# Strassen's weight sums by accumulating DMA in a transformer block's MLP on one Trainium2 core

## The chip, the cores and the metric

The kernel runs on one core of one Trainium2 chip. Its time is the device time of that core in microseconds; the number for a kernel is the median of several runs. Engines are named as in the profile: PE multiplies matrices, DVE and POOL do elementwise work, ACT does copies and functions, SP issues transfers. Each has its own queue of instructions, which it works off in order; they wait for one another by semaphores.

## The reference

One layer of a flow-matching backbone on 640 tokens (128 of a prompt, 512 of an image) of width 1024: a mixer (neighbourhood attention and a gated DeltaNet), then an MLP. Only the MLP matters here; its hidden width is 4096.

```python
def _ffn_sub(x, shift, scale, gate, w_pre, w_post, w1, w2):
    h = _rms(x, w_pre) * (1 + scale) + shift
    f = jnp.square(jax.nn.relu(h @ w1)) @ w2
    return x + gate * _rms(f, w_post)
```

## The kernel before

Everything is in fp32, and every product is made of three: each operand is split into a rounded part (hi, a cast on ACT) and a rest (lo, a subtraction on DVE), and hi·hi, hi·lo and lo·hi are added up in a PSUM bank. `split` (lines 165 to 172) does it for a weight tile of 128 x 1024, line 170 the cast and line 171 the subtraction, into one of four pairs of buffers (`whi`, `wlo`).

The MLP begins at line 1113. The 4096 hidden features go in eight groups of 512. For each group, `ff1` makes the hidden features from all tokens and `ff2` multiplies them by their rows of the second matrix and adds the result to sums `R` in SBUF. Both use Winograd's form of Strassen's scheme: the weights of a group are four quadrants, 512 KB each, and seven products of sums of quadrants take the place of eight plain ones. The plain way is used for the first product of group 0 (`ff1_first`), the second product of group 7 (in the code at the end, under the pool `fin`), and the prompt's tokens (`prompt` in `ff2`).

The loop at line 1294 runs `ff1(g)`, then `ff2(g-1)`, then `fops` of group g's features, which makes the operands of the next `ff2`: four sums of feature quadrants on POOL (lines 1224 to 1230) and their splits. So one turn of the loop, called a group here, holds a whole `ff1` and a whole `ff2`: 168 matrix instructions of 128 x 320 and 108 of 128 x 512.

Per group four quadrants are loaded for each half (line 162, SP's queue) into a pool of five `raw` buffers. Sums of quadrants are made by `sm` on POOL (line 1125): S1, S2 and S3 in `ff1`, T1, T2 and T3 in `ff2`, and the fourth forms S4 and T4 in place of S2 and T2 (lines 1197 and 1268). They lie in two buffers named `sm` that rotate. `ff1_first` uses the same two buffers eight times for its relu (`rl`, lines 1145 to 1149). DVE adds each product to what it belongs to: line 1178 for `ff1`, line 1241 (`collect`, into `R`) for `ff2`; `done` (line 1174) squares the relu.

The order on each engine is set by a scheduler that simulates the program when it is built; the code's order is its starting point. The program up to the MLP is the same in both kernels.

Of the kernel before, what the change touches and what calls it, by code (L numbers as in the profile page):

```python
# [18 lines left out]
P = 128  # L19
# [11 lines left out]
# packed constants: name -> (pack, offset, width); pack 1 is used at the start only  # L31
# [65 lines left out]
def body(ctx: ExitStack, tc: tile.TileContext, I, O, dbg=None):  # L97
# [41 lines left out]
    def newton_rsqrt(pool, x, n, tag, post=1.0):  # L139
        """1/sqrt(x) for x [P, n] > 0, times post."""  # L140
# [14 lines left out]
    behind = []  # loads wait for this one's issue  # L155
    rawp = [None, 0]  # the stage's pool for raw weights, and its buffers
# [8 lines left out]
    def split(raw, kt, n, pool=None, eng=V):  # L165
        """[P, kt, n] as the sum of two float32r parts"""
        pool = pool or wpool
        hi = pool.tile([P, 1024], F32R, tag="whi", name="whi")
        lo = pool.tile([P, 1024], F32R, tag="wlo", name="wlo")
        S.copy(hi, raw)  # L170
        eng.tensor_tensor(lo, raw, hi.bitcast(F32), op=ALU.subtract)  # L171
        return [x.rearrange("p (k n) -> p k n", k=kt) for x in (hi, lo)]
# [4 lines left out]
    def load_tok(src, n, pool=None):  # L177
        """a weight block whose columns stream: by input tile (hi, lo)"""
# [7 lines left out]
    def mm3(out, pairs):  # L186
        """out = sum of a^T b over (a_hi, a_lo, b_hi, b_lo)."""
# [24 lines left out]
    def ada_rows(c, pool):  # L212
        """256 columns of the modulation as rows: partial sums at partitions 32g + r."""
# [11 lines left out]
    def ada_cols(c, kk, dst, bcol, nsel, pool):  # L225
        """shift and (1 + scale) * norm_pre of features kk*128..+128 as columns"""
# [9 lines left out]
    def ada_gate(which, j, pool):  # L236
        """gate rows times the weight of the norm to DRAM"""
# [10 lines left out]
    def gate_bcast(which, pool):  # L248
        """(g + b) * norm_post over the partitions: [P, group, 1024]"""
# [38 lines left out]
    ab = cv.tile([P, 64], F32, tag="ab", name="ab")  # a_log, dt_bias, exp(a_log)  # L288
    cw = cv.tile([P, 60], F32, tag="cw", name="cw")

    with tc.tile_pool(name="xp", bufs=1, side="right") as xp:
        # x for now where the queries and keys will be, by halves of the features; scaled and
        # transposed to where the values will be and to a tile of the stage
# [4 lines left out]
        with tc.manual_schedule(engines={mybir.EngineType.SP}):  # L298
# [22 lines left out]
            # features as the modulation comes in; each one's products with w_z go out at once  # L321
# [42 lines left out]
    rawp[:] = [cv, 4]  # L364
    behind.append(lastd[0])
    # z: token-major, times dn_norm and its silu (twice)
# [8 lines left out]
    # b, a: features on 32 partitions, four partial sums side by side; then token-major  # L375
# [20 lines left out]
    # beta and g  # L396
# [8 lines left out]
    # softplus(x) = max(x, 0) + 2 atanh(u / (2 + u)), u = exp(-|x|)  # L405
# [25 lines left out]
    # cumulative decays  # L431
# [26 lines left out]
    # q, k, v: feature-major projection, convolution, silu, token-major  # L458
# [6 lines left out]
    for x in range(3):  # L465
# [32 lines left out]
        if x < 2:  # L498
            # values carry a factor 2 from the silu
# [45 lines left out]
    def transpose4(src, out, ps=None):  # L545
        """[tok, (a, d)] to [d, a, tok]"""
# [5 lines left out]
    def transpose8(src, tag):  # L552
        """[tok, (h, dir, d)] to [(dir, d), h, tok]"""
# [8 lines left out]
    def decay(m, d, mv, stat, lower):  # L562
        """exp of the sum of g over the open/closed run between p and f; exactly 0 outside the triangle"""
# [31 lines left out]
    def prep(mf, mb, buf):  # L595
        """everything of a pair of (tile, direction) units that doesn't need the state"""
# [3 lines left out]
        for d, m in ((0, mf), (1, mb)):  # L600
            known = m in seen  # the products of a tile serve both directions
# [5 lines left out]
            # upper: j on partitions, i >= j on columns  # L607
# [22 lines left out]
        # keys and queries times the decay from the chunk's start (and beta backward), both directions side by side  # L630
# [13 lines left out]
        Y = dp.tile([P, 16, 16], F32, tag="Yd", name="Yd")  # (column, unit)  # L644
# [8 lines left out]
        # packed: the diagonal 32 x 32 block of each row  # L653
# [7 lines left out]
        # 16 -> 32: Y12 = -Y11 U12 Y22 (the first 16 rows of U's block hold U12)  # L661
# [17 lines left out]
        # 32 -> 64  # L679
# [34 lines left out]
    def step(si, pr, St, first, last=False):  # L714
        """one chunk of both directions; St: [P (dir, dk), h, dv] or None for zero"""
# [3 lines left out]
        # right sides: v forward, beta v backward  # L719
# [37 lines left out]
        # output: q S and (q k^T) v_new  # L757
# [24 lines left out]
    def finish_o(ot, hv):  # L782
        """rms norm over each head, times dn_norm and the silu of z; feature-major to DRAM"""
# [60 lines left out]
    def fill():  # L844
        """dense work beside the DeltaNet"""
# [4 lines left out]
    def ahead(f, offset, *args):  # L850
        """f's instructions go before waiting ones of the filler"""
# [44 lines left out]
    with (  # L896
# [26 lines left out]
        for hp in range(HP):  # L923
# [3 lines left out]
            for mi in range(2):  # L927
# [5 lines left out]
                if mi == 0:  # L933
                    qb = at0.tile([P, T], F32, tag="qb", name="qb")  # context, then blocks of 16 columns
# [10 lines left out]
            # blocks of 16 columns of the grid, then the context  # L945
            for b in range(5):
                nk = 384 if b < 4 else 128
                po_ = None
                for hq in range(2):
# [7 lines left out]
                    if b < 4:  # L957
# [9 lines left out]
                        # negative scores and their minimum  # L967
# [28 lines left out]
    TG = [(0, 3), (3, 5)]  # token tiles side by side  # L996
# [7 lines left out]
    def load_wo(n, pool):  # L1004
        """the next n pieces of w_out: (hi, lo) by input tile, in fours"""
# [5 lines left out]
    if True:  # L1011
# [7 lines left out]
        for i in (1, 0):  # L1019
            if i == 0:  # L1020
# [4 lines left out]
                # m (and later h2 in its place): by token tile  # L1025
# [4 lines left out]
            for c in range(4):  # L1030
# [3 lines left out]
                for mi in range(2):  # L1034
# [3 lines left out]
                    for t0, t1 in TG:  # L1038
# [5 lines left out]
                        # twice the sigmoid times the branch  # L1044
# [8 lines left out]
    # output projection (of twice the merged branches), residual, second norm: by token tiles  # L1053
# [4 lines left out]
    with (  # L1058
# [6 lines left out]
        for t in range(5):  # L1065
# [28 lines left out]
            for kk in range(2):  # L1094
# [3 lines left out]
                # h2 takes the place of m  # L1098
# [347 lines left out]
```

## Time and profile before

| | us |
|---|---|
| median of 3 runs (1233.77 to 1238.07) | 1233.88 |
| span of the profiled execution | 1234.3 |
| DVE busy in it | 948.5 |
| POOL busy in it | 493.2 |
| ACT busy in it | 478.7 |

A row of the page's fifth part reads: line, engine, operation, output <- inputs, shape, count, then busy time, mean of one, and the idle time of the engine just before such instructions with what ended it. L171 stands for every weight split, whatever stage it belongs to; the tile on the right of the arrow (`raw`, `S`, `T`) tells whether a plain quadrant or a sum was split. The two costliest groups of the MLP on DVE and POOL:

```
L171 DVE TENSOR_TENSOR wlo<-T,whi 128x1024 fp32r<-128x1024 f32 x28 | 54.4, 1947 | 0.6 <-ACT whi L170 0.6
L1125 POOL TENSOR_TENSOR T<-raw 128x1024 f32<-128x1024 f32 x14 | 37.1, 2651 | 68.5 <-DVE wlo L171 37.8
```

### The profile page before, as it was taken

To read this page: it belongs to the slowest core of one execution; us is meant where nothing else is said; L and a number is where in the kernel's file an instruction comes from. 1 tells how busy PE (TensorE), PEld (TensorE's weight loads), DVE (VectorE), ACT (ScalarE), POOL (GpSimd) and SP (SyncE) were. 2 spreads that over 40 slices of the span, in tenths; PEclk is the share of its full clock that TensorE was granted. 3 is DMA by queue.
4 is the path that set the end of the run, shared out by engine and by line. 5 is a ranking of instruction groups with operands and counts; after the bars stand their busy time and mean duration, and the time that the engine had idled before them with its cause. 6 is when DMAs were issued, how large, how long until landed. Compare 5 with 4: busy or idle time off the path is not lost. (4 is left out here: it accounts for less than half of the span.)

```text
span 1234.3 us, 24857 instructions
## 1 busy us (share of the span) xinstructions
PE 1132.2 (92%) x10111; PEld 993.8 (81%) x10111; DVE 948.5 (77%) x1689; ACT 478.7 (39%) x910; POOL 493.2 (40%) x322
## 2 busy tenths in 40 slices
PE   5999799899989899898999899989989989898896
PEld 3789799778777788887877899988878879796875
DVE  6568996575677675735655667899999999999996
ACT  5434344342423233224435253545443434344322
POOL 1442425150542110402310415756564656556555
PEclk9999999898989899999999999989999999999999
DMA  9721033434425433645332562022213123221405
GB/s 337 266 93 50 1 102 133 149 129 137 144 77 176 141 109 111 215 132 194 98 104 105 178 246 102 18 71 67 85 52 103 57 81 103 69 86 52 155 33 136
DMA packets 61313, 144.87 MB, mean 117 GB/s; under 512 B 12384, under 2 KB 26000, under 8 KB 61200
## 3 DMA queue, kind: packets, MB, share of 16 engines
q1 hardware_dynamic: 38528, 108.66, 26.0%
q10 hardware_dynamic: 22672, 34.64, 9.0%
q8 instruction: 79, 1.29, 0.4%
q14 instruction: 34, 0.28, 0.1%
HBM read 122.02 MB, written 21.25 MB: 116 GB/s over the span
## 5 line engine op out<-in xcount | busy, mean ns | idle before, releaser
L190 PE MATMUL ps_mm<-hhi,whi 128*128 128x320 f32 x576 | 186.8, 324 | 2.5 <-DVE gbn L244 2.0
L192 PE MATMUL ps_mm<-hhi,wlo 128*128 128x320 f32 x576 | 183.5, 319 | 0.3 <-issue 0.3
L191 PE MATMUL ps_mm<-hlo,whi 128*128 128x320 f32 x576 | 183.5, 319 | 0.0
L171 DVE TENSOR_TENSOR wlo<-raw,whi 128x1024 fp32r<-128x1024 f32 x94 | 154.3, 1650 | 31.9 <-ACT whi L170 31.4
L170 ACT CAST whi<-raw 128x1024 fp32r<-128x1024 f32 x117 | 121.4, 1047 | 112.8 <-PE ps_mm L191 26.5
L190 PEld LDWEIGHTS ps_mm<-hhi,whi 128*128 128x128 f32 x576 | 112.2, 195 | 8.0 <-DVE gbn L244 2.4
L191 PEld LDWEIGHTS ps_mm<-hlo,whi 128*128 128x128 f32 x576 | 112.1, 195 | 0.5
L192 PEld LDWEIGHTS ps_mm<-hhi,wlo 128*128 128x128 f32 x576 | 111.9, 194 | 0.6
L171 POOL TENSOR_TENSOR wlo<-raw,whi 128x1024 fp32r<-128x1024 f32 x23 | 56.9, 2477 | 81.8 <-ACT whi L170 81.5
L1125 POOL TENSOR_TENSOR T<-raw 128x1024 f32<-128x1024 f32 x14 | 37.1, 2651 | 68.5 <-DVE wlo L171 37.8
L962 POOL TENSOR_SCALAR bias<-bias 128x256 f32<-128x256 f32 x24 | 25.1, 1055 | 76.2 <-DMA bias<-in_bias_dram 72.4
L171 DVE TENSOR_TENSOR wlo<-T,whi 128x1024 fp32r<-128x1024 f32 x28 | 54.4, 1947 | 0.6 <-ACT whi L170 0.6
L170 ACT CAST whi<-T 128x1024 fp32r<-128x1024 f32 x28 | 29.4, 1052 | 63.8 <-PE ps_st L1168 19.6
L480 DVE SCALAR_TENSOR_TENSOR y<-cvb,cw,y 128x644 f32<-128x644 f32 x48 | 49.2, 1025 | 0.7
L567 POOL TENSOR_TENSOR W<-cst,ghi 128x512 fp32r<-128x512 f32 x15 | 19.0, 1265 | 73.9 <-PE ps_tp L568 71.9
L1125 POOL TENSOR_TENSOR S<-raw 128x1024 f32<-128x1024 f32 x14 | 34.2, 2440 | 33.6 <-DVE wlo L171 33.6
L1241 DVE TENSOR_TENSOR R<-R,ps_tp 128x512 f32<-128x512 f32 x64 | 42.6, 676 | 2.5 <-PE ps_tp L192 2.3
L1169 PE MATMUL ps_st<-mhi,wlo 128*128 128x320 f32 x128 | 39.2, 309 | 0.4 <-DVE wlo L171 0.4
L1168 PE MATMUL ps_st<-mlo,whi 128*128 128x320 f32 x128 | 39.4, 308 | 0.0
L1167 PE MATMUL ps_st<-mhi,whi 128*128 128x320 f32 x128 | 39.3, 309 | 0.0
L170 ACT CAST whi<-S 128x1024 fp32r<-128x1024 f32 x28 | 29.2, 1047 | 24.8 <-POOL S L1125 24.8
L651 DVE TENSOR_TENSOR tq<-tq,Ud 128x16 f32<-128x16 f32 (+14 forms) x75 | 35.7, 476 | 1.9
(594 smaller groups left out, 3556.3 us busy)
## 6 DMA issues: line engine op xcount, KB each, us to landing
raw<-in_w_ff_dram SPq DMA_DIRECT2D x64, 512.0 KB
raw<-in_w_ada_dram SPq DMA_DIRECT2D x48, 512.0 KB
raw<-in_w_gate_dram SPq DMA_DIRECT2D x16, 512.0 KB
raw<-in_w_dn_dram SPq DMA_DIRECT2D x12, 512.0 KB
gt_d<-gth SPq DMA_DIRECT2D x32, 160.0 KB
gl<-gt_d ACTq DMA_DIRECT2D x16, 320.0 KB
raw<-in_w_qk_dram SPq DMA_DIRECT2D x8, 512.0 KB
raw<-in_w_br_dram SPq DMA_DIRECT2D x8, 512.0 KB
```

Source lines behind the costliest of these rows:

```text
L170: S.copy(hi, raw)
L171: eng.tensor_tensor(lo, raw, hi.bitcast(F32), op=ALU.subtract)
L190: PE.matmul(out, ah, bh, start=(i == 0), stop=False)
L191: PE.matmul(out, ah, bl, start=False, stop=False)
L192: PE.matmul(out, al, bh, start=False, stop=(i == n - 1))
L480: V.scalar_tensor_tensor(y, b[:, j : j + 644], cw[:, mt * 5 + j : mt * 5 + j + 1], y, op0=ALU.mult, op1=ALU.add)
L651: V.tensor_tensor(tq[:, q:, :], tq[:, q:, :], Ud[:, :, q].unsqueeze(1).to_broadcast([P, w, 16]), op=ALU.mult)
L1125: G.tensor_tensor(x, a, b, op=op)
L1167: PE.matmul(o, hi[:, k, fs], bh, start=(k == 0), stop=False)
L1168: PE.matmul(o, hi[:, k, fs], bl, start=False, stop=False)
L1169: PE.matmul(o, lo[:, k, fs], bh, start=False, stop=(k == 3))
L1241: V.tensor_tensor(dst, dst, ps, op=ALU.add)
```

## The change

The sums of weight quadrants are no longer made on POOL. `summed` starts a tile with a plain copy of one quadrant (line 1131, SP's queue), and `plus` adds further quadrants to it by transfers that accumulate into the tile (line 1127, issued from POOL's queue, straight from DRAM). As a transfer can add but not subtract, some sums are formed with the opposite sign, and the instructions behind them subtract where they added (or take a min where they took a max). A tile carries a chain: in `ff1`, S1 is W21 + W22, is split, gets W11 added, is split again, gets W12 added and is split a third time; T1 goes the same way in `ff2`. S3 and T3 are two quadrants each. The products are reordered so that each form is used in the order in which the chain makes it. A wait for the splits that read a form stands ahead of each further addition. `raw` loads fall from eight to seven per group, since W21 of `ff1` is needed in sums alone. The rest of the diff takes comments out. Its core:

```diff
-    def sm(name, a=None, b=None, op=None):
-        x = fa.tile([P, 1024], F32, tag="sm", name=name, bufs=2)
-        if a is not None:
-            G.tensor_tensor(x, a, b, op=op)
+    def sm(name):
+        return fa.tile([P, 1024], F32, tag="sm", name=name, bufs=2)
+
+    def plus(x, src):
+        nc.gpsimd.dma_start(x, src, accum_op=ALU.add)
+
+    def summed(name, *srcs):
+        x = sm(name)
+        nc.sync.dma_start(x, srcs[0])
+        for src in srcs[1:]:
+            plus(x, src)
         return x
...
     def ff1(g):
-        A11, A21, A22, A12 = [load_raw(I["w_ff1"][g, i]) for i in range(4)]
+        W11, W21, W22, W12 = [I["w_ff1"][g, i] for i in range(4)]
+        S1 = summed("S1", W21, W22)
+        S3 = summed("S3", W21, W11)
+        A11, A12, A22 = [load_raw(x) for x in (W11, W12, W22)]
...
-        p = prod(A11, B11)
+        w5 = split(S1, 4, 256)
+        plus(S1, W11)
+        p = prod(split(A11, 4, 256), B11)
         for s in range(2):
             S.copy(u2[:, s], p[s])
-        add(c11, u2, prod(A12, B21))
+        add(c11, u2, prod(split(A12, 4, 256), B21))
         done(c11)
-        S1 = sm("S1", A21, A22, ALU.add)
-        S2 = sm("S2", S1, A11, ALU.subtract)
-        add(u2, u2, prod(S2, TT[1]))
-        p = prod(S1, TT[0])
-        S3 = sm("S3", A11, A21, ALU.subtract)
-        add(u3, u2, prod(S3, TT[2]))
-        add(u2, u2, p)
-        add(c22, u3, p)
-        done(c22)
-        add(u3, u3, prod(A22, B12))
-        done(u3)
-        G.tensor_tensor(S2, A12, S2, op=ALU.subtract)
-        add(u2, u2, prod(S2, B22))
+        w6 = split(S1, 4, 256)
+        plus(S1, W12)
+        add(u2, u2, prod(w6, TT[1]), ALU.subtract)
+        add(u3, u2, prod(split(S3, 4, 256), TT[2]))
+        p = prod(w5, TT[0])
+        add(u2, u2, p, ALU.subtract)
+        add(c22, u3, p, ALU.subtract)
+        done(c22, ALU.min)
+        add(u3, u3, prod(split(A22, 4, 256), B12), ALU.subtract)
+        done(u3, ALU.min)
+        add(u2, u2, prod(split(S1, 4, 256), B22))
         done(u2)
...
     def ff2(g, f):
-        B11, B21, B12, B22 = [w2_raw(g, *q) for q in ((0, 0), (1, 0), (0, 1), (1, 1))]
+        W11, W21, W12, W22 = [w2(g, *q) for q in ((0, 0), (1, 0), (0, 1), (1, 1))]
+        T1 = summed("T1", W12, W11)
+        T3 = summed("T3", W22, W12)
+        B11, B21, B22, B12 = [load_raw(x) for x in (W11, W21, W22, W12)]
...
-        T1 = sm("T1", B12, B11, ALU.subtract)
-        prod(4, "S1", split(T1, 2, 512))
-        T2 = sm("T2", B22, T1, ALU.subtract)
-        prod(5, "S2", split(T2, 2, 512))
-        G.tensor_tensor(T2, B21, T2, op=ALU.subtract)
-        prod(3, "A22", split(T2, 2, 512))
-        T3 = sm("T3", B22, B12, ALU.subtract)
-        prod(6, "S3", split(T3, 2, 512))
+        w4 = split(T1, 2, 512)
+        plus(T1, W22)
+        prod(4, "S1", w4)
+        prod(6, "S3", split(T3, 2, 512))
+        w5 = split(T1, 2, 512)
+        plus(T1, W21)
+        prod(5, "S2", w5)
         b22 = split(B22, 2, 512)
         prod(2, "S4", b22)
         prompt(1, split(B12, 2, 512, eng=G), b22)
+        prod(3, "A22", split(T1, 2, 512))
```

In `fops` two of the four sums change their sign, and the last sums over `R` (line 1312) stay seven in number with other operands and signs.

What stands in POOL's queue in a turn of the loop (the third) before: the weight sums, T for `ff2` and S for `ff1`, one split (L171) and the four sums of `fops` (tiles named c).

```order
L1125 TENSOR_TENSOR T1_11074<-raw_11016,raw_11012 128x1024
L1125 TENSOR_TENSOR T2_11096<-raw_11018,T1_11074 128x1024
L1125 TENSOR_TENSOR T3_11139<-raw_11018,raw_11016 128x1024
L1268 TENSOR_TENSOR T2_11096<-raw_11014,T2_11096 128x1024
L1125 TENSOR_TENSOR S1_11318<-raw_11243,raw_11245 128x1024
L1125 TENSOR_TENSOR S2_11320<-S1_11318,raw_11241 128x1024
L171 TENSOR_TENSOR wlo_11182<-raw_11016,whi_11181 128x1024
L1224 TENSOR_TENSOR c22_10774<-c12_10772,c22_10774 128x2x256
L1226 TENSOR_TENSOR c12_10772<-c11_10771,c12_10772 128x2x256
```

The same turn in POOL's queue after the change; a row with DMA is the issue of one accumulating transfer.

```order
L1127 DMA T1_11011<-in_w_ff2_dram 128x1024
L1127 DMA T3_11014<-in_w_ff2_dram 128x1024
L1127 DMA T1_11011<-in_w_ff2_dram 128x1024
L1127 DMA S1_11241<-in_w_ff1_dram 128x1024
L1127 DMA T1_11011<-in_w_ff2_dram 128x1024
L171 TENSOR_TENSOR wlo_11162<-raw_11023,whi_11161 128x1024
L1127 DMA S3_11244<-in_w_ff1_dram 128x1024
L1127 DMA S1_11241<-in_w_ff1_dram 128x1024
L1238 TENSOR_TENSOR c22_10778<-c12_10776,c22_10778 128x2x256
L1127 DMA S1_11241<-in_w_ff1_dram 128x1024
L1240 TENSOR_TENSOR c12_10776<-c11_10775,c12_10776 128x2x256
```

The sums have become issues at about the same places; each issue waits for the transfer before it into the same tile and for the splits that read the tile, and a sum of `fops` now stands behind three issues of `ff1`'s tiles.

DVE's queue in `ff2` of that turn, before: the splits of T1, T2 (twice) and T3 among the collections into R.

```order
L171 TENSOR_TENSOR wlo_11099<-T2_11096,whi_11098 128x1024
L1174 SCALAR_TENSOR_TENSOR c12_10772<-c12_10772 128x640
L1241 TENSOR_TENSOR R_10054<-R_10054,ps_tb_11032 128x512
L1204 TENSOR_TENSOR A11l_11210<-c11_10771,A11h_11209 128x512
L1241 TENSOR_TENSOR R_10054<-R_10054,ps_tp_11044 128x512
L1241 TENSOR_TENSOR R_10054<-R_10054,ps_tp_11052 128x512
L1204 TENSOR_TENSOR A12l_11214<-c21_10773,A12h_11213 128x512
L171 TENSOR_TENSOR wlo_11120<-T2_11096,whi_11119 128x1024
L1241 TENSOR_TENSOR R2_10055<-R2_10055,ps_tb_11060 128x512
L171 TENSOR_TENSOR wlo_11142<-T3_11139,whi_11141 128x1024
```

DVE's queue at that place after the change.

```order
L171 TENSOR_TENSOR wlo_11080<-T1_11011,whi_11079 128x1024
L1190 TENSOR_TENSOR c12_10776<-c12_10776,ps_mm_10982 128x320
L1190 TENSOR_TENSOR c12_10776<-c12_10776,ps_mm_10995 128x320
L1186 SCALAR_TENSOR_TENSOR c12_10776<-c12_10776 128x640
L171 TENSOR_TENSOR wlo_11101<-T3_11014,whi_11100 128x1024
L1258 TENSOR_TENSOR R_10053<-R_10053,ps_tp_11029 128x512
L1258 TENSOR_TENSOR R_10053<-R_10053,ps_tb_11037 128x512
L1217 TENSOR_TENSOR A11l_11210<-c11_10775,A11h_11209 128x512
L1258 TENSOR_TENSOR R_10053<-R_10053,ps_tp_11049 128x512
L1258 TENSOR_TENSOR R_10053<-R_10053,ps_tp_11057 128x512
L1217 TENSOR_TENSOR A12l_11214<-c21_10777,A12h_11213 128x512
L171 TENSOR_TENSOR wlo_11121<-T1_11011,whi_11120 128x1024
```

The split of T1's second form (the last row) follows its first form (the first row) by eleven instructions, with T3 in between; an addition into T1 lies between the two.

In SP's queue, where before only raw loads stood, the base copies now stand among them.

```order
L1131 DMA T1_10533<-in_w_ff2_dram 128x1024
L162 DMA raw_10769<-in_w_ff1_dram 128x1024
L1131 DMA T3_10536<-in_w_ff2_dram 128x1024
L162 DMA raw_10771<-in_w_ff1_dram 128x1024
L162 DMA raw_10773<-in_w_ff1_dram 128x1024
L1131 DMA S1_10763<-in_w_ff1_dram 128x1024
L162 DMA raw_11017<-in_w_ff2_dram 128x1024
```

By the waits of these rows, a T1 copy waits for the last addition into the S3 before it, and the next S1 copy for the last addition into T3: S1 and T3 share one of the two buffers, S3 and T1 the other.

More of the change, by code (lines that the diff above doesn't have):

```diff
@@ L1152, in ff1, with prod @@
     def ff1(g):
-        A11, A21, A22, A12 = [load_raw(I["w_ff1"][g, i]) for i in range(4)]
+        W11, W21, W22, W12 = [I["w_ff1"][g, i] for i in range(4)]
+        S1 = summed("S1", W21, W22)
+        S3 = summed("S3", W21, W11)
+        A11, A12, A22 = [load_raw(x) for x in (W11, W12, W22)]
         c = f_tiles()
         c11, u2, u3, c22 = c[0, 0], c[0, 1], c[1, 0], c[1, 1]
-        def prod(raw, B):
-            hi, lo = split(raw, 4, 256)
+        def prod(w, B):
+            hi, lo = w
             res = []
@@ L1223, in fops @@
         op("A22", a22)
-        eng.tensor_tensor(a22, a21, a22, op=ALU.add)
+        eng.tensor_tensor(a22, a21, a22, op=ALU.subtract)
         op("S1", a22)
@@ L1229, in fops, with w2 @@
         op("S2", a11)
-        eng.tensor_tensor(a12, a12, a11, op=ALU.subtract)
+        eng.tensor_tensor(a12, a12, a11, op=ALU.add)
         op("S4", a12)
         return res
+    def w2(g, kh, nh):
+        return I["w_ff2"][2 * g + nh, :, kh * 1024 : kh * 1024 + 1024]
     def w2_raw(g, kh, nh):
-        return load_raw(I["w_ff2"][2 * g + nh, :, kh * 1024 : kh * 1024 + 1024])
+        return load_raw(w2(g, kh, nh))
     def collect(dst, ps, first):
@@ L1311, in body @@
     tctx.close()
-    for o, a, b in ((1, 0, 1), (5, 0, 5), (6, 5, 6), (2, 5, 2), (2, 2, 4), (3, 6, 3), (4, 6, 4)):
-        G.tensor_tensor(R[o], R[a], R[b], op=ALU.add)
+    for o, a, b, op in ((1, 0, 1, ALU.add), (5, 0, 5, ALU.add), (6, 5, 6, ALU.add), (2, 2, 4, ALU.add),
+                        (2, 2, 5, ALU.subtract), (3, 6, 3, ALU.add), (4, 4, 6, ALU.subtract)):
+        G.tensor_tensor(R[o], R[a], R[b], op=op)
     with tc.tile_pool(name="fin", bufs=2, side="right", reuse_waits="tile") as fin_:
```

8 lines of the change are left out of this document (4 added, 4 removed).

## The prediction

> **What bounds the kernel now.** I read the page's busy table and its slices first, then the windows of the MLP, the waits of PE in it, and the timeline of two engines around one instruction. The edit touches nothing before the MLP, which starts at about 804 us.
>
> ```profile
> PE 1132.2 (92%) x10111; PEld 993.8 (81%) x10111; DVE 948.5 (77%) x1689; ACT 478.7 (39%) x910; POOL 493.2 (40%) x322
> PE   5999799899989899898999899989989989898896
> DVE  6568996575677675735655667899999999999996
> ```
>
> Over the whole span PE looks like the bound. From the 27th slice on DVE is a 9 everywhere, while PE falls to 8 again and again: in the MLP both are nearly full.
>
> ```profile
> 820.00:1200.00 380.00, 352.36 (x1883) 308.10 (x1883) 371.30 (x395) 153.16 (x207) 213.51 (x89) 0.99 0.25 82
> 967.70:1022.17 54.47, 50.52 (x277) 44.48 (x277) 53.66 (x60) 21.09 (x29) 30.41 (x14) 1.00 0.23 78
> 1022.17:1076.68 54.51, 50.51 (x277) 44.49 (x276) 53.71 (x60) 21.07 (x28) 30.43 (x13) 1.00 0.24 78
> ```
>
> The columns are length, then busy time of PE, PEld, DVE, ACT and POOL, granted clock, DMA share and GB/s. The second and third rows are two periods of the loop over groups: 54.5 us each, of which PE is busy 50.5 and DVE 53.7. So a group costs what DVE needs, and PE is 4.0 us behind its own work. From 820 to 1200 us PE idles 380.0 - 352.4 = 27.6 us.
>
> ```profile
> PE ps_tp L190 <- DVE R L1241: 15.0, 10, 4.3
> PE ps_tb L190 <- DVE R L1241: 8.4, 6, 2.0
> PE ps_st L1167 <- ACT c L1183: 1.4, 1, 1.4
> PE ps_st L1169 <- DVE wlo L171: 0.6, 2, 0.4
> ```
>
> PE's waits from 818 to 1180 us (total, times, longest) agree: 23.4 us of them end when DVE has at last collected a product bank into R. That is the most that a relieved DVE can give: PE is the next bound, 7% behind.
>
> Why is DVE full? Its instructions are long for a reason that stands in two engines' timelines:
>
> ```profile
> 1010.05 1.21 DVE L171 TENSOR_TENSOR wlo<-T,whi 128x1024 fp32r<-128x1024 f32 x1
> 1011.78 3.07 DVE L171 TENSOR_TENSOR wlo<-T,whi 128x1024 fp32r<-128x1024 f32 x1
> 1011.38 2.40 POOL L1125 TENSOR_TENSOR S<-raw 128x1024 f32<-128x1024 f32 x1 [3.60 <-DVE wlo L171]
> ```
>
> Start, duration, engine. The same subtraction takes 1.21 us alone and 3.07 us when POOL is inside a sum: POOL ends at 1013.78, and DVE 1.07 us after that. The one that comes second stands still until the first is through. So POOL's time falls on DVE.
>
> **What the change removes.** Per group six sums of weight quadrants leave POOL; one group's rows:
>
> ```profile
> L1125 POOL TENSOR_TENSOR T<-raw 128x1024 f32<-128x1024 f32 x2 | 5.1, 2534 | 9.8 <-DVE wlo L171 5.2 <-DMA raw<-in_w_ff_dram 4.6
> L1125 POOL TENSOR_TENSOR S<-raw 128x1024 f32<-128x1024 f32 x2 | 4.8, 2394 | 5.6 <-DVE wlo L171 5.6
> L1125 POOL TENSOR_TENSOR T<-raw,T 128x1024 f32<-128x1024 f32 x1 | 3.3, 3260 | 0.1
> L1268 POOL TENSOR_TENSOR T<-raw,T 128x1024 f32<-128x1024 f32 x1 | 2.9, 2896 | 1.2 <-DVE wlo L171 1.2
> L1197 POOL TENSOR_TENSOR S<-raw,S 128x1024 f32<-128x1024 f32 x1 | 2.4, 2397 | 3.6 <-DVE wlo L171 3.6
> L1125 POOL TENSOR_TENSOR S<-S,raw 128x1024 f32<-128x1024 f32 x1 | 2.4, 2387 | 1.2 <-issue 1.2
> ```
>
> These are eight instructions of 128x1024, 20.9 of POOL's 30.4 us. The four sums of `fops` and one split stay, 9.5 us, and go on holding DVE. What DVE gets back, by the same group's rows:
>
> ```profile
> L171 DVE TENSOR_TENSOR wlo<-raw,whi 128x1024 fp32r<-128x1024 f32 x6 | 11.8, 1972 | 0.0
> L171 DVE TENSOR_TENSOR wlo<-T,whi 128x1024 fp32r<-128x1024 f32 x4 | 7.8, 1957 | 0.0
> L171 DVE TENSOR_TENSOR wlo<-S,whi 128x1024 fp32r<-128x1024 f32 x4 | 4.9, 1216 | 0.0
> L1204 DVE TENSOR_TENSOR A11l<-c,A11h 128x512 fp32r<-128x512 f32 x1 | 2.3, 2266 | 0.0
> L1241 DVE TENSOR_TENSOR R<-R,ps_tp 128x512 f32<-128x512 f32 x10 | 6.7, 677 | 0.6 <-PE ps_tp L192 0.6
> ```
>
> 14 splits take 24.5 us and would take 14 x 1.21 = 16.9; A11l takes 2.27 where a 128x512 instruction takes 0.68. That is 9.2 us, so DVE needs about 44.5 of a group, 6 under PE's 50.5. The signs (subtract for add, min for max) keep instruction and size: nothing. The reordered last sums over R are seven as before: nothing, and the splits' casts stay on ACT, which is busy 21 of 54 us.
>
> **What it adds.** Per group 19 transfers of 512 KB in place of 8: 7 plain loads and 4 base copies on SP, 8 accumulating ones on POOL. At 0.52 MB each that is 10.0 MB in a group of 51 us, 195 GB/s; counting an addition's second operand, 27 x 0.52 = 14.2 MB, 277 GB/s. The rate itself is there, as one lone load shows:
>
> ```profile
> 1048.38 0.33 SPq L162 DMA_DIRECT2D raw<-in_w_ff_dram  x1
> 1048.38:1049.33 0.95, 0.95 (x6) 0.85 (x6) 0.92 (x3) 0.00 (x0) 0.95 (x1) 1.00 0.00 0
> 1050.83:1051.33 0.50, 0.50 (x6) 0.50 (x5) 0.50 (x2) 0.00 (x0) 0.00 (x0) 1.00 0.92 377
> 1049.33:1051.83 2.50, 2.50 (x19) 2.50 (x18) 2.46 (x5) 0.00 (x1) 1.24 (x1) 1.00 0.62 210
> ```
>
> It is issued at 1048.38, nothing moves for 0.95 us, then 2.50 us of packets, at 377 GB/s in the middle: 3.45 us in all. **No row shows an accumulating transfer.** From below it costs a plain load, 3.45 us. From above, reading the tile, reading the weights and writing back as three whole transfers in turn: 3 x 3.45 = 10.35 us. I take the plain load with its packet time doubled, because two operands are read: 0.95 + 2 x 2.50 = 5.95 us, the nearer end being the row's.
>
> The Trainium skill, Collectives: The Full Stack (The bandwidth ceiling: the fold count and why AG ≠ RS ≠ AR), says that an add in the DMA path costs no cycles of its own but two source reads, so half the rate; with the fixed 2.0 us and 436 GB/s that its page DMA: Bandwidth & Descriptors (Anatomy of one DMA) gives, an addition of 512 KB would be an estimated 4.4 us. No run here shows it yet, and by 4.4 us the sum below would be about 3 us lower.
>
> The additions of one tile wait for each other and for the splits that read it. Two tiles rotate: by the waits in the program's order S1 and T3 share one, S3 and T1 the other, so per group a tile carries 2 copies, 4 additions and 4 splits. A split is a cast on ACT and then the subtraction:
>
> ```profile
> L170 ACT CAST whi<-T 128x1024 fp32r<-128x1024 f32 x4 | 4.2, 1054 | 8.9 <-PE ps_st L1168 4.3 <-PE ps_tp L192 3.2 <-PE ps_mm L1168 1.5
> ```
>
> 1.05 + 1.21 = 2.3 us. With a for one addition the chain is 2 x 3.45 + 4a + 4 x 2.3 = 16.1 + 4a; I allow 1.5 us for each split's turn on DVE (two collections), 6.0 in all: **22.1 + 4a**. At 5.95 it is 45.9 us, under PE's 50.5: hidden under the products. It reaches PE's 50.5 at a = 7.1, and today's 54.5 at a = 8.1. Each addition stands in POOL's queue until its tile's split is through, with the sums of `fops` behind it; those feed the next `ff2`, some 25 us of `ff1` products later, which covers such a wait. On SP the base copies wait for their tile with raw loads behind them; five raw buffers cover that. If either cover goes, PE stands for the uncovered rest.
>
> The first group has no such lead. Its two tiles are those of `ff1_first`'s relu:
>
> ```profile
> 801.83 0.89 DVE L1149 TENSOR_TENSOR c<-rl 128x128 f32<-128x128 f32 x4
> 813.83 0.64 PE L1167 MATMUL ps_st<-T2h,whi 128*128 128x320 f32 x1 [2.58 <-ACT whi L170]
> ```
>
> The first tile is free at 802.7. Copy, addition, split, addition, split: 802.7 + 3.45 + 5.95 + 2.3 + 5.95 + 2.3 = 822.7, where PE's third product starts at 813.8 now. These 8.9 us are not lost whole, since the products behind then find their splits made; I count 6.
>
> **The sum.** PE's 27.6 us of idle time go, less a residue of one collection, 0.7 us, for each of seven groups (4.9), plus 6 at the start: 1234.3 - 27.6 + 4.9 + 6.0 = 1217.6, say **1217 us**. The profiled span, 1234.3, is 0.4 above the median of the three runs, 1233.9, so it needs no correction. With a at 3.45 the start costs 1 us: about 1208 with the residue, 1203 without. With a at 7.1 the start costs 8 and the groups nearly nothing more: about 1220 to 1227.
>
> **Rivals.** (1) *The additions set the pace*, which ends slower. Place: the tile's chain. Price: 4 us per group for each us of a above PE's pace; it loses from a = 8.1 on. At the upper bound a group takes 22.1 + 41.4 = 63.5 us, 9.0 more than now, six times 54: 1288 us. For it: no row shows such a transfer, and it is issued by software on POOL. Against it: the packets of a load take only 2.5 us.
> (2) *The issue is held by DVE.* POOL's own sums wait for DVE as DVE waits for them: T<-raw,T takes 3.26 where others take 2.39. If the making of an addition's transfer waits so too, a is 5.95 + 0.87 = 6.8, the chain 49.3, and with queues behind it some 5 us are lost: 1222 us. The Trainium skill, SBUF — State Buffer (Who interferes with whom), speaks of exactly such a starvation for transfers issued from GpSimd, but ties it to DVE's two-port modes and says that tensor_tensor contends only with GpSimd's reads; the 1.21 and 3.07 us above agree with the second half, and no row here shows the first.
> (3) *No change*, 1234 us: a lies near 8.1, or DVE is held by POOL's five remaining instructions as much as now, so that the change does not free it. The two split rows above speak against the latter.
>
> **Chances.** A measurement of this kernel tells 0.5%, 6 us, from no change. Forecast (1203 to 1227): 0.50. Issue held, 1222: 0.08. No change (1228 to 1240): 0.12. Additions set the pace (1241 to 1290 and beyond): 0.30. So faster 0.58, same 0.12, slower 0.30. The range takes the forecast's low end and the price at the upper bound, 1202 to 1288; about 0.15 lies outside, most of it above.
>
> **What would show it.** A period of L1238 on POOL of 51 to 52 us, DVE's 128x1024 splits near 1.2 us on average, DVE under 46 us a group, PE's waits on R gone: the first step is right. Time from an addition's issue to the split that reads it: 5 to 6.5 us says the price was right; above 8, with PE waiting for splits of S or T, says rival 1, and the sign is wrong. A third product of the first group later than 823 us shows the start mis-sized.

## The result and the profile after

The changed kernel takes **1269.8 us** (median of 4 runs, 1262.1 to 1272.6), the kernel before 1236.0 in the same comparison: a ratio of 1.0254, interval 1.0219 to 1.0290. It is 34 us slower, where 17 us faster was forecast. The profiled execution has a span of 1268.3 us. The page's busy table and its slices of it:

```profile
PE 1139.9 (90%) x10111; PEld 1006.5 (79%) x10111; DVE 867.7 (68%) x1689; ACT 479.0 (38%) x910; POOL 384.6 (30%) x322
PE   4999899889899899899998999698989898988796
DVE  6568996584859493728556577664867778776796
```

DVE has lost 81 us of work and its row of nines, as the change wanted. Yet PE gained nothing: its slices in the MLP are 8 and 9 by turns as before. DVE's splits from 820 to 1200 us, grouped by line (count, busy us, mean ns, idle time ahead and what ended it):

```profile
L171 DVE TENSOR_TENSOR wlo<-raw,whi 128x1024 fp32r<-128x1024 f32 x39 | 52.7, 1350 | 11.1 <-ACT whi L170 11.0
L171 DVE TENSOR_TENSOR wlo<-S,whi 128x1024 fp32r<-128x1024 f32 x27 | 34.4, 1289 | 39.7 <-ACT whi L170 39.7
L171 DVE TENSOR_TENSOR wlo<-T,whi 128x1024 fp32r<-128x1024 f32 x25 | 30.6, 1224 | 40.5 <-ACT whi L170 40.5
```

They come close to the forecast 1.21 us, 1.29 in the mean. What is new stands at the row's end: DVE idles 80 us ahead of the splits of S and T, for a cast on ACT. ACT's casts wait in their turn, 101 us in the same window for transfers into S and T, the rest mostly for PE. PE's waits from 820 to 1200 us have changed with it (total, times, longest):

```profile
PE ps_st L1179 <- ACT whi L170: 12.1, 4, 4.7
PE ps_tp L190 <- DVE R L1258: 7.3, 7, 1.8
PE ps_mm L1179 <- ACT whi L170: 6.4, 2, 3.3
```

The waits for R have shrunk, from 24 us to 9.5, and 18.5 us of waits for a cast have come. Instead of one full engine there is now a chain in which each waits for the other. One turn of the loop, first in the windows (length, busy PE, PEld, DVE, ACT, POOL, clock, DMA share, GB/s):

```profile
988.48:1046.04 57.56, 51.74 (x278) 46.24 (x277) 43.58 (x59) 21.13 (x29) 15.23 (x13) 0.97 0.71 174
```

then in POOL's timeline of the same 57.56 us (start, duration, in brackets the idle time ahead and its releaser; L1127 is the issue of an addition):

```profile
988.48 1.78 POOL L1127 DMA_DIRECT2D S<-in_w_ff_dram  x2 [7.89 <-DVE R L1258]
...
1001.13 0.88 POOL L1127 DMA_DIRECT2D S<-in_w_ff_dram  x1 [4.87 <-DVE wlo L171]
...
1008.27 0.88 POOL L1127 DMA_DIRECT2D T<-in_w_ff_dram  x1 [1.56 <-DVE wlo L171]
...
1021.72 0.86 POOL L1127 DMA_DIRECT2D T<-in_w_ff_dram  x1 [3.30 <-DVE wlo L171]
...
1033.05 0.86 POOL L1127 DMA_DIRECT2D T<-in_w_ff_dram  x1 [1.24 <-DVE wlo L171]
...
1046.04 1.78 POOL L1127 DMA_DIRECT2D S<-in_w_ff_dram  x2 [8.04 <-DVE R L1258]
```

The two issues at 988.48 are S3's only addition and, right behind it in the queue, S1's second. S1's is the urgent one, since PE needs that form next. ACT's, DVE's and PE's timelines show when it comes:

```profile
998.52 2.00 ACT L170 CAST whi<-S 128x1024 fp32r<-128x1024 f32 x2 [5.85 <-DMA S<-in_w_ff_dram]
```

```profile
999.60 2.36 DVE L171 TENSOR_TENSOR wlo<-S,whi 128x1024 fp32r<-128x1024 f32 x2 [4.71 <-ACT whi L170]
...
1020.21 1.22 DVE L171 TENSOR_TENSOR wlo<-T,whi 128x1024 fp32r<-128x1024 f32 x1
...
1031.53 1.23 DVE L171 TENSOR_TENSOR wlo<-T,whi 128x1024 fp32r<-128x1024 f32 x1 [1.20 <-ACT whi L170]
...
1040.73 1.23 DVE L171 TENSOR_TENSOR wlo<-T,whi 128x1024 fp32r<-128x1024 f32 x1 [2.85 <-ACT whi L170]
```

```profile
999.62 0.64 PE L1179 MATMUL ps_mm<-T2h,whi 128*128 128x320 f32 x1 [3.28 <-ACT whi L170]
```

ACT idles 5.85 us for the transfer, DVE 4.71 for ACT, PE 3.28. And S3's form, long landed, is split only behind S1's, so its tile is free at 1001.96. SP's timeline has the two copies that the tile then waits for:

```profile
1001.99 0.33 SPq L1131 DMA_DIRECT2D T<-in_w_ff_dram  x1
...
1041.99 0.33 SPq L1131 DMA_DIRECT2D S<-in_w_ff_dram  x1
```

T1's copy leaves 0.03 us after the tile is free, T1 takes its three additions, the next S3's copy leaves 0.03 us after T1's last split, and at 1046.04 the turn begins anew. So the steps of this one tile fill the turn: 988.48, 1001.99, 1008.27, 1021.72, 1033.05, 1041.99, 1046.04. Not all of it is the tile's own time. T1's first two forms land at 1014.84 and 1027.27, but their casts start only at 1018.80 and 1030.44, and ACT's idle time ahead of both ends with PE: 7.1 us of the cycle lead through PE.

PE loses more than its wait of 3.28 us. Right behind it the profile grants half the clock:

```profile
999.60:1002.40 2.80, 2.78 (x10) 2.78 (x11) 2.80 (x3) 1.44 (x2) 1.27 (x2) 0.50 0.00 0
```

Matrix instructions of 128x320 take 0.47 us there instead of 0.31. The mean clock of the turn is 0.97, where the two periods before the change had 1.00.

### The profile page after: what moved, and what is told of

Same layout as the page of the kernel before. It is cut to its first block, busy times and chain, and to the rows that moved or that the text cites. A ratio compares the mean times of both kernels' runs of the same rounds, so it can differ in the third digit from the quotient of the medians.

```text
span 1268.3 us, 25013 instructions
## 1 busy us (share of the span) xinstructions
PE 1139.9 (90%) x10111; PEld 1006.5 (79%) x10111; DVE 867.7 (68%) x1689; ACT 479.0 (38%) x910; POOL 384.6 (30%) x322
## 5 line engine op out<-in xcount | busy, mean ns | idle before, releaser
L171 DVE TENSOR_TENSOR wlo<-raw,whi 128x1024 fp32r<-128x1024 f32 x94 | 128.9, 1380 | 41.3 <-ACT whi L170 40.6
L171 POOL TENSOR_TENSOR wlo<-raw,whi 128x1024 fp32r<-128x1024 f32 x23 | 56.5, 2461 | 84.8 <-ACT whi L170 84.5
L1127 POOL DMA_DIRECT2D S<-in_w_ff_dram x28 | 24.8, 948 | 148.0 <-DMA S<-in_w_ff_dram 58.0
L171 DVE TENSOR_TENSOR wlo<-T,whi 128x1024 fp32r<-128x1024 f32 x28 | 35.5, 1267 | 49.1 <-ACT whi L170 49.1
L171 DVE TENSOR_TENSOR wlo<-S,whi 128x1024 fp32r<-128x1024 f32 x28 | 35.6, 1287 | 42.0 <-ACT whi L170 41.9
L1127 POOL DMA_DIRECT2D T<-in_w_ff_dram x28 | 24.3, 870 | 105.8 <-DVE wlo L171 34.5
L480 DVE SCALAR_TENSOR_TENSOR y<-cvb,cw,y 128x644 f32<-128x644 f32 x48 | 49.2, 1025 | 0.7
L1179 PE MATMUL ps_st<-mhi,whi 128*128 128x320 f32 x128 | 41.5, 325 | 0.0
```

What stands on the lines that cost most here:

```text
L480: V.scalar_tensor_tensor(y, b[:, j : j + 644], cw[:, mt * 5 + j : mt * 5 + j + 1], y, op0=ALU.mult, op1=ALU.add)
L1127: nc.gpsimd.dma_start(x, src, accum_op=ALU.add)
L1179: PE.matmul(o, hi[:, k, fs], bh, start=(k == 0), stop=False)
```

## The experiments

Each run's ratio is to the kernel before on the same chip (medians there 1236.9 to 1238.9 us). "A group" is the mean period of the first sum of `fops`, from its first to its sixth group in the loop, in the profiled execution. `before` and `after` name the kernel that an edit starts from.

**What the relief of DVE is worth, and what the transfers take.** e1: `before` without any of the weight sums.

```diff
-        S1 = sm("S1", A21, A22, ALU.add)
-        S2 = sm("S2", S1, A11, ALU.subtract)
+        S1, S2 = A22, A21
...
-        T1 = sm("T1", B12, B11, ALU.subtract)
+        T1 = B12
```

> The kernel of before with no sums of weight quadrants at all: each of the six sums per group is left out and one of its quadrants is split in its place, so the products and their splits stay as many. Theory R (relief): POOL's 20.9 us of sums per group are what keeps DVE full; without them a group falls from 54.5 us to PE's 50.5 to 51.5, 20 to 28 us in all: 1206 to 1216. Rival (no relief): PE has another limit just behind, or POOL's remaining sums hold DVE as before: over 1226.

1197.4 us, ratio 0.9683 (0.9644 to 0.9723). Its window:

```profile
820.00:1180.00 360.00, 355.31 (x1944) 320.36 (x1945) 303.22 (x407) 156.06 (x218) 86.39 (x42) 1.00 0.26 85
```

PE is full, and a group takes 49.2 us, less than the 50.5 that PE was "busy" before. In `before` 128x512 rows right behind a wait for R last some 500 ns, where the median is 389, so at least part of the difference is waiting that counts as busy. The relief is there, 39 us of it, more than I forecast.

e2: `before` with the eight sums on DVE itself (`G.tensor_tensor` becomes `V.tensor_tensor` at the three places).

> The kernel of before with the same eight sums per group made by DVE in place of POOL; no accumulating transfer. Theory R: a sum on POOL costs DVE a stand of up to 2.4 us, a sum on DVE 1.2 us of its own; DVE needs 44.5 (its uncontended part and what the sums of fops still hold) + 8 x 1.2 = 54.1 less the overlap, so a group takes 51 to 54.5: 1214 to 1234. Rival: POOL's sums cost DVE less than 1.2 us each, and DVE becomes longer than 54.5: above 1240.

1223.5 us, 0.9886 (0.9850 to 0.9923). The same window of `before` and of e2:

```profile
820.00:1180.00 360.00, 333.48 (x1804) 293.51 (x1804) 353.85 (x378) 146.87 (x201) 201.31 (x84) 0.99 0.26 85
```

```profile
820.00:1180.00 360.00, 344.50 (x1867) 305.69 (x1866) 342.36 (x443) 148.56 (x204) 84.33 (x34) 0.99 0.25 83
```

The fuller engine takes on eight more instructions a group and is busy 11 us *less*: what POOL's sums took from DVE by standing in its way is more than the sums cost there.

e3: `after` with plain transfers where it had accumulating ones, on the same queue with the same waits; the weight sums are left out.

```diff
-        nc.gpsimd.dma_start(x, src, accum_op=ALU.add)
+        nc.gpsimd.dma_start(x, src)
```

> The changed kernel with each accumulating transfer replaced by a plain one of the same size into the same tile, from the same place in POOL's queue; the sums are left out (the last quadrant loaded stands in the tile). Theory A (chain of coupled tiles): four additions lie on the loop's cycle of 57.6 us; if a plain one takes 4.0 to 4.5 us in place of 6.0, a group falls by 6 to 8, to about 51: 1215 to 1232, and the order of the queue still shows. Rival T (transfers compete): the second operand's traffic is what stretches copies and loads; then copies fall back to 3.5 us too and the whole loss goes: 1205 to 1212.

1221.2 us, 0.9878 (0.9813 to 0.9944), a group of 51.2 us: within theory A's bounds and above rival T's. So neither the queue, the copies, the reordered products nor the raw loads make the loss by themselves: all of it goes when a transfer is shorter. Time from issue to landing over all of L1127, of `after` and of e3:

```profile
DMA to landing us min/median/max: 5.1/6.0/11.8
```

```profile
DMA to landing us min/median/max: 3.5/4.0/10.1
```

An addition costs 2.0 us more than a load in the same place.

**Which wait turns these 2.0 us into 58.** e4: `after` with one order changed, S3's addition behind S1's second.

```diff
-        S3 = summed("S3", W21, W11)
+        S3 = sm("S3")
+        nc.sync.dma_start(S3, W21)
...
-        plus(S1, W11)
+        with tc.issue_after(plus(S1, W11)):
+            plus(S3, W11)
```

> The changed kernel with one order changed: on POOL the addition into S3 is issued behind S1's second addition, not ahead of it. Theory A: S1's second form, for which PE waits, is held 2.3 us behind S3's copy and runs beside S3's addition (9.1 us against 5.5); so 3 to 6 us per group come back, a group of 52 to 55 us: 1232 to 1250. Rival T: the transfers are as many and as long, nothing is held by the order: 1262 to 1273 as the changed kernel.

1246.2 us, 1.0070 (1.0042 to 1.0098), a group of 54.2. 24 of the 34 us come back. POOL's timeline:

```profile
1031.34 0.88 POOL L1127 DMA_DIRECT2D S<-in_w_ff_dram  x1 [6.73 <-DVE wlo L171]
1032.66 0.86 POOL L1127 DMA_DIRECT2D S<-in_w_ff_dram  x1 [0.45 <-issue]
```

S1's addition now goes first, and lands 5.1 us later instead of 9.4.

e5 (four raw buffers, a control for e6), e6 (four raw buffers, three sum tiles) and e7 (the four sums of `fops` on DVE), each on `after`:

```diff
-        return fa.tile([P, 1024], F32, tag="sm", name=name, bufs=2)
+        return fa.tile([P, 1024], F32, tag="sm", name=name, bufs=3)
```

> A control for the next run: the changed kernel with four buffers for raw quadrants in place of five, nothing else. Theory A: raw loads come early enough with four, the loop's cycle runs over the sum tiles: 1258 to 1275, as the changed kernel. Rival T: with fewer loads under way the transfers compete less or PE waits for raw quadrants more: outside of that.

> The changed kernel with three tiles for the sums, in the room of the raw buffer that the run before gives up. Theory A: S1, S3, T1 and T3 no longer wait in pairs for one another's last split; a cycle of 57.6 us over two tiles is spread over three, and the group falls to PE's pace or a little over it, 51 to 54 us: 1222 to 1245. Rival T: the same transfers in the same time: 1258 to 1275.

> The changed kernel with the four sums of fops on DVE, so that POOL's queue holds issues and one split alone. Theory A says that POOL's order holds S1 behind S3's copy, which stays here, and that the sums stand behind issues without harm: a gain of 0 to 10 us at most, from S1l and S3l that POOL's sums make long: 1258 to 1272. Rival Q (queue): sums and issues hold one another up in POOL's queue, and this is most of the loss: 1225 to 1250.

e5 1272.2 us, 1.0283 (1.0229 to 1.0336); e6 1266.9, 1.0233 (1.0187 to 1.0279); e7 1270.6, 1.0257 (1.0237 to 1.0277). None differs from `after`. For e6 that was a miss of theory A: if two tiles are the chain, a third should break it. POOL's timeline of e6 shows why it doesn't:

```profile
986.08 0.88 POOL L1127 DMA_DIRECT2D T<-in_w_ff_dram  x1 [8.21 <-DMA T<-in_w_ff_dram]
986.66 1.19 POOL L1127 DMA_DIRECT2D S<-in_w_ff_dram  x1
```

With a tile free, the next T1 starts early, and its addition takes S3's place ahead of S1's second. S1's stands in the queue until T1's copy has landed, is issued right behind T1's addition and lands at 997.15, 10.5 us after its issue. The tile was not the whole chain; the place in the queue belongs to it too.

**What is left after the order.** e8 (on `after`: first sums by transfer, the further additions into S1 and T1 on DVE, from the raw quadrants), e11 (e8 with `fops` on DVE) and e12 (e8 with the first sums of S1 and T1 on DVE too, so that only S3 and T3 are transfers):

```diff
-        plus(S1, W11)
+        V.tensor_tensor(S1, S1, A11, op=ALU.add)
...
-        plus(T1, W22)
+        V.tensor_tensor(T1, T1, B22, op=ALU.add)
```

> The changed kernel with the chain cut: S1, S3, T1 and T3 are begun by a copy and one accumulating transfer each, well ahead of their use; the two further additions into S1 and into T1 are made by DVE from the raw quadrants. Theory A: an addition between two splits of a tile costs 1.2 us in place of some 6 and the turn behind the other tile goes, DVE needs 42 + 4 x 1.2 = 47 of PE's 50.5: a group of 51 to 52.5 us, 1212 to 1228, faster than before. Rival T: four accumulating transfers and four copies per group still compete with the loads; half of the loss stays: 1245 to 1260.

> e8 (first sums by accumulating transfers, the chain's steps on DVE) with the four sums of fops on DVE instead of POOL. In e8 PE waits 3.3 us a group for ACT's copies into c (L1197), which wait for the sums of fops on POOL (4 x 2.2 us, behind an addition's issue). Theory: with these on DVE that wait goes, a group falls from 55.3 to 51.5 to 53.5 us, and the time to 1222 to 1235. Rival (DVE, at 47.5 + 4 x 0.7 = 50.3 us a group, sets the pace, or the wait moves to S1's additions): 1240 to 1246.

> e2 (sums on DVE, 58.7 of each 60 us busy) with the two sums that are no chain, S3 and T3, as accumulating transfers and signs as in the change: 2 additions and 2 copies a group in place of 8 and 4, and DVE freed of two sums, 2.4 us a group. Theory (an addition costs nothing where its tile is not written again and its issue has a group's time): a group of 51 to 52.5 us, 1210 to 1221. Rival (the additions' issue stands behind the splits and the sums of fops on POOL, and PE waits): 1224 to 1245.

e8 1244.2 us, 1.0054 (1.0036 to 1.0072), a miss, just under the rival's bounds; e11 1233.2, 0.9952 (0.9922 to 0.9982), within the theory's bounds; e12 1235.0, 0.9966 (0.9937 to 0.9995), a miss of the theory and within the rival's bounds. PE's waits from 900 to 1180 us in e8 (total, times, longest):

```profile
PE ps_st L1179 <- ACT c L1197: 9.9, 3, 3.3
PE ps_mm L1179 <- ACT c L1197: 6.6, 2, 3.3
```

In e12 the same two waits come to 23.2 us from 800 to 1225 us. In this stretch of e8 no sum tile is late; at the start e8 and e11 still have a wait of over 10 us for a cast, as `after` has, and e12 one of 3.3. PE waits for a bank of the first product, which ACT cannot copy into c, because the parts and sums of `fops` still read c's tile (ACT's own wait for c ends with DVE's S3l). In e11 these sums are on DVE and 11 us come back. e12 keeps them on POOL; whether that alone holds it back was not tried.

e9 (e4 with four raw buffers and the relu of `ff1_first` in tiles of its own) and e14 (e4 with `fops` on DVE), and both together, e15:

```diff
-                rl = sm("rl")
+                rl = fa.tile([P, 384], F32, tag="rl", name="rl", bufs=2)
...
-            f = fops(c)
+            f = fops(c, V)
```

> The order of e4 (S1's second addition issued ahead of S3's), four raw buffers, and the relu of the first group in tiles of its own, so that S1's copy of the first group need not wait for it. Theory A: the change lost 33 us in two places, about 24 by the order in POOL's queue (e4 gave them back) and about 10 at the start of the first group, where PE waited 10.3 us for S1's second form in e4. With both mended: 1234 to 1240 us, as before the change, and PE's longest wait before 850 us under 4. Rival (the start's wait only moves to a later place): 1243 to 1250, as e4.

> e4 (two tiles, S1's second addition ahead of S3's) with the four sums of fops on DVE. In e4 PE waits 9.5 us in all for ACT's copies into c and 20 us for collections into R. Theory A: the waits for c go, 1234 to 1242. Rival (two tiles hold the group at 54.2 whatever stands in POOL's queue): 1243 to 1250.

> e9 (e4 with four raw buffers and the first group's relu in tiles of its own) with the four sums of fops on DVE. In e9 the start's wait is gone, but a group takes 56.0 us where e4's takes 54.2, and PE waits 13.9 us in all for ACT's copies into c. Theory A: these waits are the sums of fops behind additions in POOL's queue; without them a group of 53 to 54.5 us and 1224 to 1234. Rival (four raw buffers slow the loads): a group stays at 55 to 56, 1238 to 1244.

e9 1241.7 us, 1.0029 (1.0002 to 1.0056); e14 1242.1, 1.0029 (1.0003 to 1.0054); e15 1226.0, 0.9900 (0.9870 to 0.9929). Each mend alone gives 4 us, which is not clear of the noise (the intervals overlap with e4's); both give 20. e9 lies between the bounds of its two theories: in e9 the start's wait is gone, but a group takes 56.0 us where e4's takes 54.2, so the gain was mostly lost again. e14's time stands at the edge of its bounds and says little alone. e15's time is within theory A's bounds, but its profiled execution is the longest of its six, with a group of 55.3 us, so that no group time can be given for the median.

e10: three tiles, S1's second addition ahead of S3's, the next T1's first behind S1's third; e13: the same with `fops` on DVE.

```diff
-        T1 = summed("T1", W12, W11)
+        T1 = sm("T1")
+        nc.sync.dma_start(T1, W12)
+        with tc.issue_after(s1l[0]):
+            plus(T1, W11)
```

> Three sum tiles with four raw buffers as in e6, and the order set by hand: S1's second addition ahead of S3's, the next T1's first addition behind S1's third. In e6 S1's second addition was issued at 986.66, right behind T1's at 986.08, and landed only at 997.15, 10.5 us later, and PE waited for it: by theory A the third tile did nothing because another addition took S3's place ahead of S1's in POOL's queue. Then this gives 1228 to 1242, with a group of 52 to 53.5 us and the start's 10 us still lost. Rival (the sharing of tiles doesn't matter at all, S1's own chain of three additions does): 1244 to 1250 as e4, a group of 54 us.

> e10 (three sum tiles, S1's second addition ahead of S3's, T1's first behind S1's third) with the four sums of fops on DVE, so that POOL's queue holds additions alone. In e10 PE waits 4.7 us a group for ACT's copies into c (L1200), ACT and DVE wait for the last sum of fops on POOL (L1247, 22.0 and 22.9 us), and that sum stands in POOL's queue behind T1's first addition. Theory A (what is left of the loss in e10 is again one instruction waiting behind another's wait in POOL's queue): a group falls from 56.3 to 51.5 to 53 us, the time to 1226 to 1240, of which the start's 10 us are still lost. Rival (the additions of S1 and T1 alone keep the group at 54 to 56): 1244 to 1256.

e10 1256.4 us, 1.0144 (1.0103 to 1.0184), a miss by both theories; e13 1227.0, 0.9922 (0.9898 to 0.9946), within theory A's bounds. PE's waits and two rows of POOL's timeline in e10:

```profile
PE ps_st L1181 <- ACT c L1200: 15.7, 4, 4.7
PE ps_mm L1181 <- ACT whi L170: 9.7, 1, 9.7
PE ps_mm L1181 <- ACT c L1200: 9.4, 2, 4.7
```

```profile
997.02 0.88 POOL L1127 DMA_DIRECT2D T<-in_w_ff_dram  x1 [3.90 <-DMA T<-in_w_ff_dram]
997.62 1.59 POOL L1247 TENSOR_TENSOR c<-c,c 128x512 f32<-128x512 f32 x1
```

The last sum of `fops` stands behind an addition (T3's; my expectation named T1's) that waits 3.90 us for its copy, and c comes free that much later. Taking the same four sums out of POOL's queue gave nothing on `after` (e7) and 29 us here: a wait shows only when the longer one beside it is gone. e13's group is 53.5 us, in a profiled execution of 1234.5 us, the longest of its seven.

e16: e13 with the relu in its own tiles, and three raw buffers to make room.

> e13 (three sum tiles, order of the additions set, fops on DVE: 1227.0 us, of which PE waits 9.3 us for S1's second form at the start) with the first group's relu in tiles of its own, and three raw buffers instead of four to make room. Theory A (the start costs its own 5 to 10 us beside the groups): 1216 to 1223. Rival (three raw buffers hold the loads back, or the start's wait moves into the groups as in part in e9): 1225 to 1240.

**1217.3 us**, 0.9850 (0.9821 to 0.9880), a group of 51.4 us, within theory A's bounds: the lowest time of the kernels that make all the sums, with the additions as dear as ever (5.0 us at least, 6.2 in the median). PE's waits from 800 to 1225 us:

```profile
PE ps_tp L190 <- DVE R L1261: 7.4, 8, 2.9
PE ps_mm L1181 <- ACT c L1200: 4.4, 3, 2.2
PE ps_st L1181 <- ACT c L1200: 3.8, 4, 1.4
PE ps_mm L191 <- DVE mlo L1105: 2.6, 1, 2.6
```

No wait on S or T is left in PE's list. That this kernel comes out at the time forecast for the change is no support of the forecast: it needed four mends. Against e2's 0.9886 its lead lies within the intervals.

## Why the prediction was wrong, step by step

**DVE is relieved: right, and too small.** I called 23.4 us the most that a relieved DVE could give, and in the sum I took all 27.6 us of PE's idle time as gone. e1 gave 39. By e1 PE's own pace is 49.2 a group and not the 50.5 of its busy time. POOL's issues don't hold DVE up again: a group's splits take 18.1 us where I had 16.9.

**The price of an addition: right.** Forecast 5.95 us, median 6.0; the four in the turn above take 5.2, 6.6, 5.5 and 6.5, together 23.8, and 4a was 23.8. The lower end, 3.45, is a plain load's 3.5. The Trainium skill, Collectives: The Full Stack (The bandwidth ceiling: the fold count and why AG ≠ RS ≠ AR), has the add of a ReduceScatter read two sources and run at half the rate of a copy. The share of DMA time by queue agrees, from 820 to 1180 us in `after` and in e3 (packets, MB, share of 16 engines):

```profile
q0 software_dynamic: 7179, 26.13, 41.2%
```

```profile
q0 software_dynamic: 7632, 27.79, 23.4%
```

That is 1.58% a MB against 0.84%, 1.9 times as much. The 4.4 us that I estimated with that page were too few, against the median of 6.0.

**The fixed part of the tile's chain: this step failed.** I wrote 22.1 + 4a. The turn took 57.56, so at 4a = 23.8 the fixed part is **33.8**, 11.7 us more:

- Two copies, 6.9 forecast, took 6.28 (1001.99 to 1008.27) and 4.05 (1041.99 to 1046.04), 10.3.
- Four splits with their turns, 9.2 + 6.0 forecast, took the remaining 23.4. My allowance was for turns on DVE alone. The largest piece is S3's: landed at 993.6, split at 1001.96, 8.3 us, because S1's form was split first and that one's addition stood *behind* S3's in POOL's queue. I gave each tile its own chain, and the queue joins the two: S3 holds S1 back, and S1 holds S3's tile. Another 7.1 us are T1's first two forms, which had landed and waited for ACT and PE (3.96 and 3.17).

With 33.8 the chain passes the old 54.5 at a = 5.2 and not at 8.1, so with it the change loses at the price that I had forecast. It is not a constant, since parts of it hang on PE's progress. In e3 it would give 33.8 + 4 x 4.0 = 49.8, near PE's own pace of 49.2, and 51.2 was measured. e4 shows the queue's part: 24 of the 34 us.

**What a wait of PE costs: left out.** I counted a wait at its own length. In the turn above PE's idle time is 5.8 us where it was 4.0, and its busy time 51.7 where it was 50.5, with 1.4 us lost in the 2.8 us at half clock alone. From 800 to 1230 us the mean granted clock is 0.95 in `after` and 0.98 in `before`. By these rounded figures that is at most an estimated 0.03 x 430 = 13 us of the 34. In the turn above the half clock follows PE's wait; no run separates its share.

**POOL's queue covered by 25 us of products: right in `after`, not in e10.** e7 shows no cost of `fops` behind the additions. In e10 the cover is gone, and taking the sums out of the queue gives 29 us.

**Raw loads behind copies on SP: no sign against it.** With one raw buffer less (e5) the interval overlaps that of `after`.

**The start: 6 us forecast, more found, and in another place.** The third product (L1179 on T2h) was to start at 822.7 and started at 826.28. But PE stands already at the first, which needs only a raw quadrant. ACT's timeline, and PE's:

```profile
814.93 1.04 ACT L170 CAST whi<-S 128x1024 fp32r<-128x1024 f32 x1 [2.35 <-DMA S<-in_w_ff_dram]
815.88 1.99 ACT L170 CAST whi<-raw 128x1024 fp32r<-128x1024 f32 x2
```

```profile
816.98 0.64 PE L1179 MATMUL ps_mm<-mhi,whi 128*128 128x320 f32 x1 [10.52 <-ACT whi L170]
```

The reordered products split S1 first. Its cast waits for the addition until 814.91, and the casts of the raw quadrants stand behind it in ACT's queue. I looked at the wait of S1's own product and not at what its cast holds. Freed, it gave 4.5 us on e4, not clear of the noise, and about 10 on e13 (e16, with a raw buffer less).

**A slip in the sum's low end.** With a at 3.45 the start costs 5 us less, so the sum with the residue is 1217.6 - 5 = about 1213 and not 1208; 1208 is without the residue, where I wrote 1203. The result lies far above either.

**The rivals.** The first, additions set the pace, came true in kind and not in its reason: I put the turning point into the price of an addition, when the unsure number was the fixed part. Its sign is there: S1's second addition was issued at 989.06 and its split began at 999.60, 10.5 us later, with PE waiting for it. The second, the issue held by DVE, falls: the issues of T take 856 to 910 ns with DVE at work, those of S 858 to 882 but for the first (1039) and six that follow right behind another (1194 to 1197). The Trainium skill's starvation (SBUF — State Buffer, Who interferes with whom) does not show here. The third, no change, falls with the 34 us; DVE was freed, to 43.6 us of the turn above.

**Still open.** e16 is 20 us above e1. PE's waits listed for e16 are 18 us; which of them bind was not separated. Why e12 is 11 us above e2 was not settled either.

## What to carry to other kernels

Before a sum is turned into accumulating transfers, write one turn of the buffer's cycle with *every* wait in it, the copy, the issue's place in its queue and the cast's place in its own, and leave several us for each turn; a sum of bare durations came out 12 us short of 58. Transfers issued from an in-order engine should be queued by who needs them first, with the urgent ones ahead of those whose tile merely came free, and with no other work of that engine behind their waits. When a mend shows nothing, read the next wait before dropping it: e7 gave nothing, and the same edit gave 29 us once the order was right. And a wait of PE should be priced above its own length: the profile's granted clock behind it belongs to the price.

## What the runs showed of the hardware

- An accumulating transfer of 512 KB issued on POOL lands after 5.1 us at least, 6.0 in the median; a plain one in the same place after 3.5 and 4.0. Its issue takes POOL 0.86 to 0.88 us in the median instead of 0.53.
- Two additions issued one right after the other land one behind the other: of those at 988.48 the first lands after 5.2 us and the second after 9.4, of those at 1046.04 after 5.2 and 9.1.
- Behind a wait of PE of 3.28 us the granted clock was 0.50 for at least 2.8 us (999.60 to 1002.40), and 128x320 matrix instructions took 0.47 us instead of 0.31.
- Moving POOL's sums onto DVE, the fuller engine, cut DVE's busy time in 360 us from 353.9 to 342.4.
